# State products of a chunked scan, and the spread of 1 / rms, in float32r passes of heads and rests

## The chip, the cores and the metric

The kernel runs on one core of one Trainium2 chip. It is one program with one launch. The metric is the device time of that core in microseconds; the median of three runs before the change is 1921.77 us. A core has TensorE (PE in the profile, with PEld for its weight loads), VectorE (DVE), ScalarE (ACT), GpSimd (POOL), and SyncE (SP), which issues most DMAs. PE multiplies out of SBUF into PSUM banks of 512 fp32 columns on 128 partitions.

## The reference

One layer of a hybrid decoder, in fp32, on a prompt of 16 meta tokens and 1024 tokens and on eight samples of one token each:

```python
h = h + 0.5 * swiglu(rmsnorm(h, n1), w1g, w1u, w1d)
u = rmsnorm(h, nm) @ w_in
q, fz, iv, g, z, xbc, dt_raw = jnp.split(u, SPLITS, axis=-1)
...
o_hg, s_hg = run_segments(hgrn2_chunked, HG_CHUNK, segs, ...)
...
y, s_ssm = run_segments(partial(ssd_chunked, a_neg=a_neg), SSM_CHUNK, segs, ...)
...
h = h + jnp.concatenate([o_hg, yz], axis=-1) @ w_out
h = h + 0.5 * swiglu(rmsnorm(h, n2), w2g, w2u, w2d)
```

Two pieces of it matter here. The first is the norm ahead of the first FFN, `y = x * rsqrt(mean(x * x) + EPS) * w`, one factor 1 / rms per token. The second is the step of the Mamba-2 scan over chunks of 128 tokens:

```python
def step(h, inp):
    xc, dtc, bc, cc = inp
    cum = jnp.cumsum(dtc * a_g, axis=1)
    ...
    y = jnp.einsum('bgts,bgrts,bsgr,bsgrp->btgrp', cb, seg, dtc, xc)
    y = y + jnp.einsum('btgn,bgrpn,btgr->btgrp', cc, h, jnp.exp(cum))
    last = cum[:, -1]
    h = (h * jnp.exp(last)[..., None, None]
         + jnp.einsum('bsgn,bsgr,bsgrp->bgrpn', bc, dtc * jnp.exp(last[:, None] - cum), xc))
    return h, y
```

There are 8 heads of 64 columns in 2 groups, and a state of 128. The sum with `bc` in the last line is the state product.

## The kernel before

The 1048 tokens lie along the free axis, in four quarters of Q = 262 columns, and the features on partitions. The five stages follow each other on PE: first FFN, input projection with both scans laid into it, output projection, second FFN, final norm.

Nearly all products of the large weights are made by `mm3`: each operand is a float32r head (a rounded copy) and a float32r rest (operand minus head), and a product is three passes into the same PSUM bank, head by head, head by rest, rest by head (L169, L170, L171). Heads of weights are cast on ACT, rests are subtracted on DVE (`split`, L163 and L164; L497 and L501 in the FFNs). A smaller number of products is made in plain fp32, which the profile counts as two records each on PE. Among them are the spread of 1 / rms and everything in the Mamba-2 scan.

Buffers: slots "u" (30) and "s" (8, of 1056 columns) for large tiles, tiles "t" (9, of 524 columns, used as fp32), PSUM banks "mis" (4, in rotation through `psm`) and "acc" (4) for the large products.

**The norm in the first FFN.** Here the factor 1 / rms isn't applied to x ahead of the products; it is multiplied into their results. `Input.rms` computes it for each token with tokens on partitions: `st[:, 1]` holds ten columns, one for each tile of 128 tokens (the last has fewer; `tiles` lists start and count). What the FFN needs is a tile whose every partition holds the factors along the free axis, the spread. For this ACT scales the identity by each of the ten columns (L1425), which gives a diagonal of 1048 columns in a "u" slot, and `spread_r(q)` multiplies a matrix of ones with a quarter of it (L1430, one fp32 product of 262 columns for each q) and copies the bank to SBUF on ACT (L1431). The FFN's products are a numbered list of steps; `before(S, i, ...)` puts other work ahead of step i, and `spread_r(q)` stands ahead of step 28 + q. L704 and L705 later consume a spread quarter on DVE and ACT.

**The scan.** `ssm_scan` handles nine chunks c, eight of 128 tokens and one of 16. `front(c)` prepares, `back(c, hT)` consumes, and `fill(n)` issues n steps of the input projection, each three float32r passes of 344 to 350 columns, between them. After two fronts the loop is back(c), front(c + 2), fill(10). In `front`: a DMA brings the cumulated decays of eight heads, one row on all partitions, into a slot "s" (`mt`, L1612) and another brings `ec` (L1619); PE transposes x into bank px (L1622) and B into bank pb (L1630), and multiplies B by C into the other half of pb (L1632); DVE makes `xdt` (L1627), the masked product (L1633) and `xw` (L1641); ACT copies B transposed out of pb (`bt`, L1634) and turns `mt` into decays by eight Relus and an Exp (L1637, L1638); DVE multiplies these by the masked product (L1640, two instructions); ACT applies Exp to `ec` (L1643). In `back`: C by the state into bank pi (L1654), which DVE multiplies into `ec` (L1655); the y product from `xdt` and `mt` into bank py (L1659), added by DVE (L1662); the state product from `bt` and `xw` into bank ps, two fp32 products of 128 x 256 (L1665); the old state by its decay (L1670) and the sum (L1671) on DVE; the skip term (L1674). So a chunk takes five "mis" banks of four.

The order of PE's instructions in this part is the one written in the code. The order on the other engines is decided by a scheduler from the program's dependences.

Of the kernel before, what the change touches and what calls it, by code (L numbers as in the profile page):

```python
# [9 lines left out]
F32 = mybir.dt.float32  # L10
F32R = mybir.dt.float32r
U8 = mybir.dt.uint8
AF = mybir.ActivationFunctionType
# [4 lines left out]
P = 128  # L18
# [6 lines left out]
T = TP + NS  # L25
# [3 lines left out]
Q = T // 4  # L29
# [38 lines left out]
class Core:  # L68
# [45 lines left out]

    def t(self, w=CW):
        t = self.tmp.tile([P, 2 * Q], F32, tag="t", name=self.uid("t"), bufs=9)
        return t[:, :w]

    def raw(self, w=512):
# [175 lines left out]
class Spread:  # L295
# [14 lines left out]
    def lanes(self, n, cs):  # L310

        return self.tile().rearrange("p (c n t) -> p n c t", c=2, n=2)[:, n, cs]
# [896 lines left out]
def constants(K, a):  # L1209
    nc = K.nc  # L1210
    cst = K.const
    K.ident = cst.tile([P, P], F32, name="ident")
    make_identity(nc, K.ident)
    K.ones = {}
    for n in (1, D):
        K.ones[n] = cst.tile([P, P], F32, name=f"ones{n}")
        nc.vector.memset(K.ones[n], 1.0 / n)
    K.eps = cst.tile([P, 1], F32, name="eps")
    nc.vector.memset(K.eps, EPS)
    K.lna = cst.tile([P, 1], F32, name="lna")  # L1220
    nc.vector.memset(K.lna, -math.log(2.0) / 3.0)
# [85 lines left out]
class Input:  # L1307
# [111 lines left out]
    def rms(self):  # L1419

        K = self.K
        token_rstd(K, *(self.st[:, j] for j in range(3)))
        self.diag = K.slot("u", T)
        for i, (t0, n) in enumerate(self.tiles):
            K.nc.scalar.activation(self.diag[:, t0 : t0 + n], K.ident[:, :n], AF.Identity, scale=self.st[:, 1, i : i + 1])  # L1425

    def spread_r(self, q):
        K = self.K
        ps = K.psm()[:, :Q]
        K.nc.tensor.matmul(ps, K.ones[1], self.diag[:, q * Q : q * Q + Q], start=True, stop=True)  # L1430
        K.nc.scalar.copy(self.spread.quarter(q), ps)  # L1431


def token_rstd(K, v, r, q):

    token_sqrt(K, v, r)
    token_newton(K, v, r, q)
# [162 lines left out]
def ssm_scan(K, a, o, fill):  # L1600
    nc = K.nc
# [3 lines left out]
    state = {}  # L1605

    def front(c):

        t0, n = CT[c]
        r8 = slice(8 * c, 8 * c + 8)  # L1610
        mt = K.slot("s", w=1024).rearrange("p (h t) -> p h t", h=8)
        nc.sync.dma_start(mt[:, :, :n], K.cumd[r8, :n].partition_broadcast(P))  # L1612
        tk = K.pack()
        ec, bt, cbm = tk.tile([P, 4, P]), tk.tile([P, 256]), tk.tile([P, 2, P])
        cs = slice(t0, t0 + n)
        if c > 0:

            for f in range(2):
                nc.sync.dma_start(ec[64 * f : 64 * f + 64, :, :n], K.cumd[8 * c + f : 8 * c + 8 : 2, :n].partition_broadcast(64))  # L1619
        px = K.psm()  # L1620
        for j in range(4):
            nc.tensor.transpose(px[:n, j * P : (j + 1) * P], xs[j][:, cs], K.ident)  # L1622
        xx = K.slot("s", w=1024)
        xdt = xx[:, 0:512]
        xw = xx[:, 512:1024]
        pxv = px[:n].rearrange("p (h d) -> p h d", h=8)
        nc.vector.tensor_mul(xdt[:n].rearrange("p (h d) -> p h d", h=8), pxv, K.dt[:n, r8][:, :, None].broadcast_to([n, 8, 64]))  # L1627
        pb = K.psm()
        for g in range(2):
            nc.tensor.transpose(pb[:n, g * P : (g + 1) * P], B[g][:, cs], K.ident)  # L1630
        for g in range(2):
            nc.tensor.matmul(pb[:n, 256 + g * P : 256 + g * P + n], B[g][:, cs], C[g][:, cs], start=True, stop=True)  # L1632
        nc.vector.tensor_mul(cbm[:n, :, :n], pb[:n, 256:512].rearrange("p (g t) -> p g t", g=2)[:, :, :n], K.tri[:n, None, :n].broadcast_to([n, 2, n]))  # L1633
        nc.scalar.copy(bt[:n], pb[:n, 0:256])  # L1634

        for hh in range(8):
            nc.scalar.activation(mt[:n, hh, :n], mt[:n, hh, :n], AF.Relu, scale=-1.0, bias=K.cum[:n, 8 * c + hh : 8 * c + hh + 1])  # L1637
        nc.scalar.activation(mt[:n, :, :n], mt[:n, :, :n], AF.Exp, scale=-1.0)  # L1638
        for g in range(2):
            nc.vector.tensor_mul(mt[:n, 4 * g : 4 * g + 4, :n], mt[:n, 4 * g : 4 * g + 4, :n], cbm[:n, g, None, :n].broadcast_to([n, 4, n]))  # L1640
        nc.vector.tensor_mul(xw[:n].rearrange("p (h d) -> p h d", h=8), pxv, K.wdec[:n, r8][:, :, None].broadcast_to([n, 8, 64]))  # L1641
        if c > 0:
            nc.scalar.activation(ec[:, :, :n], ec[:, :, :n], AF.Exp)  # L1643
        state[c] = mt, ec, bt, xdt, xw

    def back(c, hT):
        t0, n = CT[c]
        r8 = slice(8 * c, 8 * c + 8)
        cs = slice(t0, t0 + n)
        mt, ec, bt, xdt, xw = state.pop(c)  # L1650
        if c > 0:
            pi = K.psm()
            for j in range(4):
                nc.tensor.matmul(pi[:, j * P : j * P + n], hT[:, j * P : (j + 1) * P], C[j // 2][:, cs], start=True, stop=True)  # L1654
            nc.vector.tensor_mul(ec[:, :, :n], pi.rearrange("p (j t) -> p j t", j=4)[:, :, :n], ec[:, :, :n])  # L1655
        py = K.psm()
        for hh in range(8):
            j, f = divmod(hh, 2)
            nc.tensor.matmul(py[64 * f : 64 * f + 64, j * P : j * P + n], xdt[:n, 64 * hh : 64 * hh + 64], mt[:n, hh, :n], start=True, stop=True)  # L1659
        pyv = py.rearrange("p (j t) -> p j t", j=4)  # L1660
        if c > 0:
            nc.vector.tensor_add(ec[:, :, :n], pyv[:, :, :n], ec[:, :, :n])  # L1662
        ps = K.psm()
        for g in range(2):
            nc.tensor.matmul(ps[:, 256 * g : 256 * g + 256], bt[:n, g * P : (g + 1) * P], xw[:n, 256 * g : 256 * g + 256], start=True, stop=True)  # L1665
        hn = hbuf[c % 2]
        if c == 0:
            nc.scalar.copy(hn, ps)
        else:
            nc.vector.tensor_mul(hn.rearrange("p (h d) -> p h d", h=8), hT.rearrange("p (h d) -> p h d", h=8), K.ecl[:, r8][:, :, None].broadcast_to([P, 8, 64]))  # L1670
            nc.vector.tensor_add(hn, hn, ps)  # L1671
        for j in range(4):
            yj = ec[:, j, :n] if c > 0 else pyv[:, j, :n]
            nc.vector.scalar_tensor_tensor(xs[j][:, cs], xs[j][:, cs], K.dcol[:, j : j + 1], yj, ALU.mult, ALU.add)  # L1674
        return hn

    fill(14)
    front(0)
    fill(6)
    front(1)  # L1680
# [544 lines left out]
def body(ctx, tc, a, o):  # L2225
    nc = tc.nc
    K = Core(ctx, tc)
# [6 lines left out]
    x = Input(K, a, wn1, ops, spread)  # L2234

    def before(S, i, *fns):
        for fn in fns:
            S.before(i, (lambda fn=fn: fn[0](*fn[1:])))

    def first1(S, w, w2):  # L2240
# [73 lines left out]
        before(S, 27, (e.low, 5), (e.cast, 7))  # L2314
        before(S, 28, (e.low, 7))
        for q in range(4):
            before(S, 28 + q, (x.spread_r, q))
        before(S, 33, (e.cast, 4))
        before(S, 34, (e.low, 4))

# [59 lines left out]
    with K.tc.manual_schedule(engines={mybir.EngineType.PE}):  # L2380
# [9 lines left out]
        for hd in range(NH):  # L2390
# [4 lines left out]
            g = us[hd]["g"] if hd < 3 else None  # L2395
# [29 lines left out]
    for k in range(KT):  # L2425
        t = K.slot("s", TO)
# [141 lines left out]
```

## Time and profile before

| | before |
|---|---|
| three runs, us | 1921.77, 1921.94, 1921.77 |
| profiled execution, us | 1922.67 |
| its span, us | 1920.9 |
| mean granted PE clock | 0.998 |
| PE idle while the scan runs (814 to 886 us), by the windows | 0.04 us |
| the four spread products, from the last pass ahead of them to the first one behind, us | 59.77 to 68.92 |

The span is the time from the first to the last instruction on the core; the time of a run has a little more around it. A row of a timeline is start, duration, engine, line, operation, output and inputs by the program's names, shapes and count; in brackets stands the idle time of the engine ahead of it and what ended it. PE's instructions are pipelined, so their durations overlap, and the time that one occupies PE is read from the distance between starts. Rows of PEld are the weight loads that run ahead of the matmuls. A row of the groups by line ends with the busy time, the mean duration in ns, and the idle time ahead of it.

### The profile page before, as it was taken

How to read it: one execution, taken by the hardware profiler on the slowest of the kernel's cores; microseconds unless marked ns; L12 is line 12 of the kernel's file. 1: busy time of each engine (PE TensorE's matmuls, PEld its weight loads, DVE VectorE, ACT ScalarE, POOL GpSimd, SP SyncE). 2: the span in 40 equal slices, each digit the busy share in tenths (PEclk: the TensorE clock that was granted, in tenths of full speed). 3: DMA queues.
4: the chain of work that ended last, by engine and by line, in shares of the span. 5: the costliest groups of instructions: out<-in, count | busy, mean ns of one | idle time of the engine just before them, and what ended most of it. 6: DMA issues, size and time to landing. Idle time of an engine off the chain costs nothing.

```text
span 1920.9 us, 41195 instructions
## 1 busy us (share of the span) xinstructions
PE 1905.5 (99%) x16692; PEld 1875.2 (98%) x16692; DVE 1526.5 (79%) x2866; ACT 858.0 (45%) x1635; POOL 30.1 (2%) x88
## 2 busy tenths in 40 slices
PE   9999999999999999999999999999999999999998
PEld 9999999999999999999999999999999999999998
DVE  7888888889788877566585557999888888978974
ACT  6533333334534644466564545743333332453353
POOL 3000000000000000000000000000000000000000
PEclk9999999999999999999999999999999999999999
DMA  7143333335967541221463254133333333596852
GB/s 249 50 128 95 95 107 112 92 98 175 305 215 243 165 152 52 66 89 38 116 186 85 83 173 144 58 114 107 99 93 101 101 112 93 173 269 210 281 175 84
DMA packets 324209, 258.46 MB, mean 135 GB/s; under 512 B 18923, under 2 KB 298731, under 8 KB 324011
## 3 DMA queue, kind: packets, MB, share of 16 engines
q1 hardware_dynamic: 323779, 255.79, 43.1%
q8 instruction: 131, 2.15, 0.5%
q14 instruction: 59, 0.48, 0.1%
q0 software_dynamic: 224, 0.04, 0.0%
q10 hardware_dynamic: 16, 0.00, 0.0%
HBM read 190.79 MB, written 65.05 MB: 133 GB/s over the span
## 4 chain that ended last, share of the span: by engine, by line
PE 94%; DVE 3%; ACT 1%; issue 1%; DMA 0%; SPq 0%; DVEq 0%; ACTq 0%
PE acc L169 24%; PE acc L171 23%; PE acc L170 23%; PE mis L169 5%; PE mis L170 5%; PE mis L171 5%; PE mis L1963 1%; DVE u L382 1%; DVE u L367 1%; PE mis L1665 0%; PE mis L2030 0%; PE mis L1659 0%; DMA s<-in_x_prompt_dram 0%; PE mis L2055 0%; PE mis L1654 0%
## 5 line engine op out<-in xcount | busy, mean ns | idle before, releaser
L169 PE MATMUL acc<-u,ws 128*128 128x258 f32 (+4 forms) x3634 | 1064.0, 293 | 1.1 <-DVE u L1279 0.8
L171 PE MATMUL acc<-u,ws 128*128 128x258 f32 (+4 forms) x3634 | 1055.3, 290 | 0.7 <-DVE ws L501 0.7
L170 PE MATMUL acc<-u,ws 128*128 128x258 f32 (+4 forms) x3634 | 1054.8, 290 | 0.0
L169 PEld LDWEIGHTS acc<-u,ws 128*128 128x128 f32 x3634 | 686.5, 189 | 8.7 <-issue 6.2
L170 PEld LDWEIGHTS acc<-u,ws 128*128 128x128 f32 x3634 | 688.3, 189 | 0.8 <-DVE u L330 0.2
L171 PEld LDWEIGHTS acc<-u,ws 128*128 128x128 f32 x3634 | 686.1, 189 | 1.6 <-DVE ws L501 1.1
L169 PE MATMUL mis<-u,ws 128*128 128x262 f32 (+1 forms) x810 | 230.2, 284 | 0.0
L171 PE MATMUL mis<-u,ws 128*128 128x262 f32 (+1 forms) x810 | 228.7, 282 | 0.0
L170 PE MATMUL mis<-u,ws 128*128 128x262 f32 (+1 forms) x738 | 208.6, 283 | 0.0
L501 DVE TENSOR_TENSOR ws<-r,ws 128x512 fp32r<-128x512 f32 x266 | 181.6, 684 | 4.1 <-ACT ws L497 3.9
L901 ACT ACTIVATE t<-t 128x524 f32<-128x524 f32 (+1 forms) x72 | 46.1, 640 | 300.1 <-DVE t L898 300.1
L497 ACT CAST ws<-r 128x512 fp32r<-128x512 f32 x266 | 156.8, 615 | 42.2 <-PE mis L171 18.1
L169 PEld LDWEIGHTS mis<-u,ws 128*128 128x128 f32 x810 | 152.9, 189 | 0.1
L171 PEld LDWEIGHTS mis<-u,ws 128*128 128x128 f32 x810 | 152.7, 189 | 0.0
L170 PEld LDWEIGHTS mis<-u,ws 128*128 128x128 f32 x738 | 139.9, 190 | 0.1
L493 DVE TENSOR_TENSOR r<-r,r 128x512 f32<-128x512 f32 x150 | 100.8, 684 | 0.3
L1031 DVE TENSOR_TENSOR u<-u,u 128x1048 fp32r<-128x1048 f32 (+3 forms) x84 | 96.1, 1146 | 4.8 <-ACT u L1027 4.3
L1089 ACT CAST ws<-u 128x512 fp32r<-128x512 f32 (+1 forms) x72 | 42.1, 585 | 109.9 <-DVE u L1084 105.2
L164 DVE TENSOR_TENSOR ws<-r,ws 128x512 fp32r<-128x512 f32 x88 | 59.5, 685 | 38.3 <-ACT ws L163 38.0
L1027 ACT CAST u<-u 128x1048 fp32r<-128x1048 f32 (+3 forms) x84 | 82.8, 988 | 1.3 <-DMA u<-hd 1.3
L1118 DVE SCALAR_TENSOR_TENSOR s<-acc,s 128x524 f32<-128x524 f32 (+3 forms) x86 | 53.9, 651 | 35.3 <-PE acc L171 35.0
L898 DVE TENSOR_TENSOR t<-t,u 128x524 f32<-128x524 f32 (+1 forms) x108 | 73.2, 692 | 0.1
(465 smaller groups left out, 2329.1 us busy)
## 6 DMA issues: line engine op xcount, KB each, us to landing
r<-in_w_ffn_down_dram SPq DMA_DIRECT2D x128, 256.0 KB
hd<-s SPq DMA_DIRECT2D x93, 258.0 KB
r<-in_w_ffn_gate_dram SPq DMA_DIRECT2D x88, 256.0 KB
r<-in_w_ffn_up_dram SPq DMA_DIRECT2D x88, 256.0 KB
hd<-s SPq DMA_DIRECT2D x77, 262.0 KB
u<-hd SPq DMA_DIRECT2D x36, 516.0 KB
u<-hd SPq DMA_DIRECT2D x28, 524.0 KB
r<-in_w_in_dram SPq DMA_DIRECT2D x56, 256.0 KB
```

Source lines behind the costliest of these rows:

```text
L164: self.nc.vector.tensor_sub(lo, src, hi.bitcast(F32))
L169: mm(ps, whi, xhi, start=first, stop=False, skip_group_check=more)
L170: mm(ps, whi, xlo, start=False, stop=False, skip_group_check=more)
L171: mm(ps, wlo, xhi, start=False, stop=last, skip_group_check=more)
L493: self.K.nc.vector.tensor_tensor(self.raw[p], self.raw[x], self.raw[y], op)
L497: self.K.nc.scalar.copy(self.w[p][:, : self.n * P], self.raw[p])
L501: self.K.nc.vector.tensor_sub(t[:, 512 : 512 + w], self.raw[p], t[:, :w].bitcast(F32))
L898: nc.vector.tensor_mul(t, t if src is None else src, spread.lanes(n, slice(0, 2)))
L901: nc.scalar.activation(t, t, AF.Silu)
L1027: K.nc.scalar.copy(hi, lo.bitcast(F32))
L1031: K.nc.vector.tensor_sub(lo, lo.bitcast(F32), hi.bitcast(F32))
L1118: nc.vector.scalar_tensor_tensor(t, b, 0.5, t, ALU.mult, ALU.add)
```

## The change

It edits two places. In the scan, `bt`'s head and rest lie side by side in one "t" tile declared float32r (`tr`), the rest by a new DVE subtraction out of pb; `xw` is split into `xh` (ACT) and `xl` (DVE), each in a "t" tile; and the state product is `mm3` for each of the two groups, six float32r passes of 256 columns. In the first FFN, the ten scaled identities go. The ten columns of 1 / rms are split into heads and rests in one small tile (`parts`, two DVE operations), and a spread quarter is made of passes with a column of `parts`, repeated over 128 columns, as weights, and of columns of a float32r identity (`identr`, cast once on DVE at the start) as the moving side: for each piece of a token tile in the quarter one pass for the head and one for the rest, 24 in all. They stand ahead of step 29 + q.

```diff
+    def tr(self, w=512):
+        t = self.tmp.tile([P, 2 * Q], F32R, tag="t", name=self.uid("t"), bufs=9)
+        return t[:, :w]
...
+    K.identr = cst.tile([P, P], F32R, name="identr")
+    nc.vector.tensor_copy(K.identr, K.ident)
...
-        self.diag = K.slot("u", T)
-        for i, (t0, n) in enumerate(self.tiles):
-            K.nc.scalar.activation(self.diag[:, t0 : t0 + n], K.ident[:, :n], AF.Identity, scale=self.st[:, 1, i : i + 1])
+        self.parts = K.sml.tile([P, 2, 10], F32R, tag="rp", name="rp", bufs=1)
+        K.nc.vector.tensor_copy(self.parts[:, 0], self.st[:, 1])
+        K.nc.vector.tensor_sub(self.parts[:, 1], self.st[:, 1], self.parts[:, 0].bitcast(F32))
 
     def spread_r(self, q):
         K = self.K
         ps = K.psm()[:, :Q]
-        K.nc.tensor.matmul(ps, K.ones[1], self.diag[:, q * Q : q * Q + Q], start=True, stop=True)
+        for i, (t0, n) in enumerate(self.tiles):
+            c0, c1 = max(t0, q * Q), min(t0 + n, q * Q + Q)
+            for j in range(2):
+                if c0 < c1:
+                    K.nc.tensor.matmul(ps[:, c0 - q * Q : c1 - q * Q], self.parts[:, j, i : i + 1].broadcast_to([P, P]), K.identr[:, c0 - t0 : c1 - t0], start=j == 0, stop=j == 1)
         K.nc.scalar.copy(self.spread.quarter(q), ps)
...
-        ec, bt, cbm = tk.tile([P, 4, P]), tk.tile([P, 256]), tk.tile([P, 2, P])
+        ec, cbm = tk.tile([P, 4, P]), tk.tile([P, 2, P])
+        bt, xh, xl = K.tr(), K.tr(), K.tr()
...
-        nc.scalar.copy(bt[:n], pb[:n, 0:256])
+        nc.scalar.copy(bt[:n, 0:256], pb[:n, 0:256])
+        nc.vector.tensor_sub(bt[:n, 256:512], pb[:n, 0:256], bt[:n, 0:256].bitcast(F32))
...
+        K.split(xw[:n], xh[:n], xl[:n])
...
         for g in range(2):
-            nc.tensor.matmul(ps[:, 256 * g : 256 * g + 256], bt[:n, g * P : (g + 1) * P], xw[:n, 256 * g : 256 * g + 256], start=True, stop=True)
+            gs, xs_ = slice(g * P, g * P + P), slice(256 * g, 256 * g + 256)
+            K.mm3(ps[:, xs_], bt[:n, gs], bt[:n, 256 + g * P : 256 + g * P + P], xh[:n, xs_], xl[:n, xs_], True, True)
...
-            before(S, 28 + q, (x.spread_r, q))
+            before(S, 29 + q, (x.spread_r, q))
```

The line numbers grow by the change: L1622 becomes L1633, L1630 L1641, L1640 L1652, L1641 L1653, L1655 L1668, L1659 L1672, L1430 L1440, and the passes of `mm3` become L173 to L175.

PE at the first spread quarter; `mis_886` and `mis_893` are its bank, the other rows are the FFN's passes. Before:

```order
L169 MATMUL mis_871<-u_438,ws_609 128x262
L170 MATMUL mis_871<-u_491,ws_609 128x262
L171 MATMUL mis_871<-u_438,ws_609 128x262
L1430 MATMUL mis_886<-u_814,ones_83 128x262
L169 MATMUL acc_825<-u_526,ws_628 128x262
```

With the change:

```order
L173 MATMUL acc_819<-u_528,ws_630 128x262
L174 MATMUL acc_819<-u_546,ws_630 128x262
L175 MATMUL acc_819<-u_528,ws_630 128x262
L1440 MATMUL mis_893<-identr,rp 128x128 x4
L1440 MATMUL mis_893<-identr,rp 128x6 x2
L173 MATMUL acc_833<-u_528,ws_647 128x262
```

One product is six passes, and it stands behind all twelve passes of the next step.

PE in a middle chunk of the scan, from the last pass of a fill over C by the state (`u`, `s`) and the y product to the state product. Before:

```order
L171 MATMUL acc_10355<-u_8548,ws_10069 128x350
L1654 MATMUL mis_10368<-u_9776,s_9903 128x128 x2
L1654 MATMUL mis_10368<-u_9877,s_9903 128x128 x2
L1659 MATMUL mis_10374<-s_10203,s_10213 64x128 x8
L1665 MATMUL mis_10384<-s_10213,s_10205 128x256 x2
```

With the change:

```order
L175 MATMUL acc_10411<-u_8562,ws_10095 128x350
L1667 MATMUL mis_10424<-u_9790,s_9917 128x128 x2
L1667 MATMUL mis_10424<-u_9891,s_9917 128x128 x2
L1672 MATMUL mis_10430<-s_10243,s_10256 64x128 x8
L173 MATMUL mis_10440<-t_10247,t_10246 128x256
L174 MATMUL mis_10440<-t_10248,t_10246 128x256
L175 MATMUL mis_10440<-t_10247,t_10246 128x256
```

The last three come once more, for the second group. Nothing else moves here: six passes that read "t" tiles stand where the two fp32 products stood.

DVE in the same part, from the two multiplications of a front (xdt and xw, out of px) to the two additions of the back behind it. Before:

```order
L1627 TENSOR_TENSOR s_10314<-mis_10309,s_8936 128x512
L1641 TENSOR_TENSOR s_10314<-mis_10309,s_8936 128x512
L1670 TENSOR_TENSOR s_9903<-s_9903,s_8936 128x512
L164 TENSOR_TENSOR ws_10529<-r_10527,ws_10529 128x512
L1640 TENSOR_TENSOR s_10304<-s_10304,s_10306 128x512 x2
L1655 TENSOR_TENSOR s_10205<-mis_10368,s_10205 128x512
L1662 TENSOR_TENSOR s_10205<-mis_10374,s_10205 128x512
L1671 TENSOR_TENSOR s_9903<-s_9903,mis_10384 128x512
```

With the change:

```order
L1646 TENSOR_TENSOR t_10357<-mis_10369,t_10357 128x256
L1638 TENSOR_TENSOR s_10367<-mis_10362,s_8950 128x512
L1653 TENSOR_TENSOR s_10367<-mis_10362,s_8950 128x512
L1684 TENSOR_TENSOR s_9917<-s_9917,s_8950 128x512
L168 TENSOR_TENSOR ws_10600<-r_10598,ws_10600 128x512
L168 TENSOR_TENSOR ws_10605<-r_10603,ws_10605 128x512
L1652 TENSOR_TENSOR s_10354<-s_10354,s_10356 128x512 x2
L168 TENSOR_TENSOR t_10359<-s_10367,t_10358 128x512
L1668 TENSOR_TENSOR s_10245<-mis_10424,s_10245 128x512
L1685 TENSOR_TENSOR s_9917<-s_9917,mis_10440 128x512
L1675 TENSOR_TENSOR s_10245<-mis_10430,s_10245 128x512
```

New are the rest of bt (L1646) and the rest of xw (L168 into a "t" tile). The latter stands between L1652, which was L1640, and L1668, which was L1655; it does so in this chunk, the one ahead and the one behind, and in no other chunk do these three follow each other so. The sum into the state (L1685) and the addition of y (L1675) have changed places.

More of the change, by code (lines that the diff above doesn't have):

```diff
@@ L1641, in front @@
         nc.vector.tensor_mul(xw[:n].rearrange("p (h d) -> p h d", h=8), pxv, K.wdec[:n, r8][:, :, None].broadcast_to([n, 8, 64]))
+        K.split(xw[:n], xh[:n], xl[:n])
         if c > 0:
             nc.scalar.activation(ec[:, :, :n], ec[:, :, :n], AF.Exp)
-        state[c] = mt, ec, bt, xdt, xw
+        state[c] = mt, ec, bt, xdt, xh, xl
     def back(c, hT):
@@ L1649, in back @@
         cs = slice(t0, t0 + n)
-        mt, ec, bt, xdt, xw = state.pop(c)
+        mt, ec, bt, xdt, xh, xl = state.pop(c)
         if c > 0:
```

## The prediction

> **What bounds the kernel now.** I read the page first: shares of busy time, then the chain that ended last.
>
> ```profile
> span 1920.9 us, 41195 instructions
> PE 1905.5 (99%) x16692; PEld 1875.2 (98%) x16692; DVE 1526.5 (79%) x2866; ACT 858.0 (45%) x1635; POOL 30.1 (2%) x88
> PE 94%; DVE 3%; ACT 1%; issue 1%; DMA 0%; SPq 0%; DVEq 0%; ACTq 0%
> ```
>
> TensorE (PE) is busy for 99% of the span, and the chain runs through it for 94%. So an edit pays by the PE time that it takes out, and costs by the PE idle time that it makes. The list of what PE waited for tells how little idle time there is to win.
>
> ```profile
> PE mis L1343 <- DMA s<-in_x_prompt_dram: 2.1, 2, 1.9
> PE acc L105 <- DVE ws L101: 1.5, 1, 1.5
> ```
>
> These lead that list and lie in the load at the start, which the change leaves alone. Of the rest only this group, from the groups by line and shape, belongs to what it edits: 0.9 us of waiting, last column.
>
> ```profile
> L1430 PE MATMUL mis<-u,ones 128*128 128x262 f32 x8 | 2.6, 410 | 0.9 <-ACT u L1431 0.5 <-ACT u L1425 0.4
> ```
>
> The other place that it edits, the scan, was read from the table of nine-us windows and then from the timeline. Its fullest window:
>
> ```profile
> 868.00:877.00 9.00, 9.00 (x73) 8.55 (x74) 8.39 (x17) 8.22 (x15) 0.00 (x0) 1.00 0.27 89
> ```
>
> The columns behind the width are PE, weight loads, DVE, ACT, POOL. PE is full there, but DVE and ACT come within 0.6 and 0.8 us of it. Here work added on DVE and ACT can turn into a PE wait.
>
> **The state products.** One chunk on PE, in the timeline:
>
> ```profile
> 842.15 1.13 PE L1665 MATMUL mis<-s,s 128*128 128x256 f32 x4
> 843.12 0.60 PE L1622 MATMUL mis<-ident,u 128*128 128x128 f32 x4
> 843.56 0.41 PE L1630 MATMUL mis<-ident,u 128*128 128x128 f32 x2
> ```
>
> Records overlap, so I price by distance from start to start. Two fp32 products take 843.12 - 842.15 = 0.97 us. Six float32r passes of 256 columns replace them. The nearest row is the same kind of pass at 262 columns, in the first FFN:
>
> ```profile
> 59.77 0.28 PE L171 MATMUL mis<-u,ws 128*128 128x262 f32 x1
> 60.45 0.71 PE L1430 MATMUL mis<-u,ones 128*128 128x262 f32 x2 [0.40 <-ACT u L1425]
> 60.81 0.48 PE L169 MATMUL acc<-u,ws 128*128 128x262 f32 x1
> 61.12 0.29 PE L170 MATMUL acc<-u,ws 128*128 128x262 f32 x1
> ...
> 62.34 0.28 PE L171 MATMUL acc<-u,ws 128*128 128x262 f32 x1
> 62.46 0.60 PE L1430 MATMUL mis<-u,ones 128*128 128x262 f32 x2
> 62.71 0.48 PE L169 MATMUL acc<-u,ws 128*128 128x262 f32 x1
> 63.02 0.29 PE L170 MATMUL acc<-u,ws 128*128 128x262 f32 x1
> ...
> 68.92 0.28 PE L169 MATMUL acc<-u,ws 128*128 128x262 f32 x1
> ```
>
> From 61.12 to 62.34 lie ten passes, 0.122 us each. Six times that by 256/262 is 0.72, plus up to 0.1 for the turn from fp32 to float32r: a gain of 0.15 to 0.25 per chunk. I take 0.2, and for nine chunks (the last is as dear, its moving side being 256 wide too) **1.8 us** of PE.
>
> The new work lies on ACT and DVE. The rows nearest in shape:
>
> ```profile
> 859.77 0.63 ACT L163 CAST ws<-r 128x512 fp32r<-128x512 f32 x1
> 861.39 0.68 DVE L164 TENSOR_TENSOR ws<-r,ws 128x512 fp32r<-128x512 f32 x1
> 864.23 0.42 DVE L1633 TENSOR_TENSOR s<-mis,tri 128x256 f32<-128x256 f32 x1
> ```
>
> So a chunk adds 0.63 on ACT (xh) and 0.68 + 0.42 on DVE (xl, the rest of bt). bt's head was a copy before as well. None of the three is wanted soon: the state product that reads them comes a chunk later. By throughput there is room except in the window shown. What matters is who queues behind xl.
>
> That is L1655. It reads pi, and pi's PSUM bank (four in rotation, five taken per chunk) is the next one that pb's transposes (L1630) need. On DVE, L1655 stands behind L1640, which stands behind the Relu and Exp of a matrix that a DMA brings into the slot freed by the y product one chunk back. The loop, in rows:
>
> ```profile
> 850.03 1.09 PE L1659 MATMUL mis<-s,s 128*64 128x128 f32 x16
> 851.06 1.13 PE L1665 MATMUL mis<-s,s 128*128 128x256 f32 x4
> 851.22 0.33 SPq L1612 DMA_DIRECT2D s<-cumd  x1
> 855.36 0.40 ACT L1637 ACTIVATE s<-s,s 128x128 f32<-128x128 f32 x1 [4.87 <-DMA s<-cumd]
> 855.66 0.35 ACT L1634 COPY s<-mis 128x256 f32<-128x256 f32 x1
> 858.50 1.05 ACT L1638 ACTIVATE s<-s 128x1024 f32<-128x1024 f32 x1
> 859.58 1.29 DVE L1640 TENSOR_TENSOR s<-s,s 128x512 f32<-128x512 f32 x2 [2.93 <-ACT s L1638]
> 860.79 0.68 DVE L1655 TENSOR_TENSOR s<-mis,s 128x512 f32<-128x512 f32 x1
> 860.89 0.60 PE L1622 MATMUL mis<-ident,u 128*128 128x128 f32 x4
> 861.53 0.44 PE L1630 MATMUL mis<-ident,u 128*128 128x128 f32 x2
> PEld mis L1630 <- DVE s L1655: 0.3, 1, 0.3
> ```
>
> The y product ends at 851.06 and the loop lets L1630 go at 861.53: 10.47 us. By PE alone L1630 would come at 860.89 + 0.44 = 861.33 (four transposes took 843.12 to 843.56): 10.27. So the cover is already gone in this chunk, where L1630 waits 0.2 us; the last row, from the weight loads' waits, names the same wait and releaser.
>
> After the change PE's side of that race holds two state products, each 0.2 shorter: 10.27 - 0.4 = 9.87. The loop's side gains xl, 0.6 at DVE's distance (860.79 to 861.39 for an operation of 0.68), and loses some 0.2, since bt's copy (855.66) stands ahead of the Relus, in ACT's wait for the DMA: about 10.85. The order puts xl between L1640 and L1655 (there L1652 and L1668) in three consecutive chunks and in none of the others whose race is this close. A wait of 0.7 to 1.0 gives PE's side of the following chunk that much more, so every second one pays: two waits, 1.6 together. The 0.2 of before is taken off: **1.4 us** comes back. Bounds: none, if the DMA lands earlier or the scheduler's slack holds; three full waits, 3.0, if no chunk is relieved by the one ahead. Net of the scan: -1.8 + 1.4 = **-0.4**, between -2.3 (0.25 each, no wait) and +1.65 (0.15 each, three waits).
>
> The fills are queued behind a waiting L1630 on PE, and ACT and DVE get their drains later; nobody else waits. The tiles for bt, xh and xl come from a ring of nine that holds three chunks, and a chunk's are read at most two chunks after they are taken, so I cost the ring at nothing.
>
> **The spread.** From the last pass before it (59.77) to L169 at 68.92 are 9.15 us. That holds 49 distances of float32r passes, 49 x 0.122 = 5.98, so the four products with their waits cost 3.17. Where L1430 didn't wait it took 63.02 - 62.46 - 0.122 = 0.44; 4 x 0.44 = 1.76, and the rest, 1.4, is waiting for the diagonal (0.4) and for the copy L1431 (0.5, both in the group's row), with the restart behind each. Why both came late:
>
> ```profile
> 59.15 0.17 DVE L1451 TENSOR_TENSOR st<-st 128x10 f32<-128x10 f32 x1
> 59.41 2.84 ACT L1425 ACTIVATE u<-ident,st 128x128 f32<-128x128 f32 x10 [1.16 <-DVE st L1451]
> 64.58 0.38 ACT L1431 COPY u<-mis 128x262 f32<-128x262 f32 x1 [0.41 <-PE acc L171]
> 70.67 0.70 DVE L704 TENSOR_TENSOR t<-t,u 128x524 f32<-128x524 f32 x1
> ```
>
> Ten activations held ACT for 2.84 us. The change replaces them by two DVE operations of some 0.17 each (the L1451 row), ready by 59.8, and the first product moves one step, twelve passes or 1.5 us, later. Both waits go. What replaces the fp32 products is 24 small passes, 16.4 units of 128 columns if the narrow ones are added up. Their price has no row. Low end: streaming alone, 0.06 for 128 columns, 16.4 x 0.06 = 1.0. High end: fp32's price, 0.97 / 4 = 0.24 per 128 columns, 3.9. Each pass brings its own 128 columns of weights, as the transposes do, which have 128 columns too and run at 0.44 / 4 = 0.11; C·h, 16 columns wide in the last chunk, has a group of its own:
>
> ```profile
> L1654 PE MATMUL mis<-u,s 128*128 128x16 f32 x8 | 1.0, 252 | 0.0
> ```
>
> 8 records in 1.0 us, 0.125 each, however narrow. I take the transposes' 0.11: 24 x 0.11 = 2.64, a gain of 3.17 - 2.64 = **0.5 us**; by the ends +2.2 and -0.7. The last copy, to end near 69.5, is wanted by L704 at 70.67: the step's delay costs nothing, and a copy later than that would push the DVE chain behind it. The float32r identity is one more cast on DVE in the load at the start, where the first products wait for DMA; at nothing, and 0.2 us if that cover is gone.
>
> The Trainium skill bears on the price of these passes: "TensorE: Matmul & The Clock Gate", section "LDWEIGHTS (loading the stationary operand)", gives a load as its columns / 1.2 ns, whatever the rows. An estimate by it is 107 ns for 128 columns, 2.6 us for 24 loads. It speaks against splitting four products into 24, and the 0.11 of the transposes agrees with it.
>
> **Sum.** -0.4 - 0.5 = -0.9: span 1920.0. The runs' median 1921.77 stands 0.87 above the span of the profiled execution (1920.9), and I keep that distance: **1920.9 us**.
>
> **Rivals.** *All of PE's gain stays.* The loop doesn't get longer where it counts, since L1655 is released earlier by a Relu chain without bt's copy: -1.8 - 0.5, less the 0.2 wait that exists: 1919.3, and with every cheap end (0.25 per chunk, 2.2) 1917.1. For it: the wait stands once in the scan today. Against: the order has xl ahead of L1655 in the chunk behind that very one.
>
> *The small passes stream.* The loads hide fully and a 128-column pass costs 0.06: the spread gains 2.2 instead of 0.5, 1919.2. For it: 48 passes around it hide theirs under 262 columns. Against: 128-column transposes don't. The Trainium skill, same page, section "Weight-path perf modes — Fast Weight Load (FWL) and DoubleRow", has fast loads on for 128 weights of a type that isn't FP32; whether float32r counts no run here shows.
>
> *Slower: L1630's bank.* xl ahead of L1655 delays every chunk's transposes instead of every second of three. Seven boundaries at 0.6 are 4.2; -1.8 - 0.5 + 4.2 = +1.9: 1923.7. It decides from waits of 2.3 us in all, the two gains together. For it: DVE's 8.39 of 9 us in the window above, with 1.1 us per chunk to come. Against: in the other boundaries the order has L1655 first or PE's slack is larger.
>
> *Not what it says.* Passes from the new tiles run at fp32's price, 0.24 per 128 columns: six of them 2.9 instead of 0.97, nine chunks +17, 1938. The operand type is the one of the 262-column rows, so hardly.
>
> **How the numbers follow.** My forecast 0.58, all gain 0.17, streaming 0.09, slower 0.14, not what it says 0.02. A run of this kernel can tell about 0.2% from no change, 3.84 us: below 1917.9 or above 1925.6. Faster by that needs nearly every cheap end of two rivals at once: 0.07. Slower needs the bank wait at twice its price, or the last rival: 0.08. Same: 0.85. The range takes in streaming with most of the gain kept below, and the bank rival above: 1917.9 to 1924.0.
>
> **What would show it.** The six passes of a chunk at 0.12 from start to start, next transposes 0.7 to 0.8 after the first. At L1641 (L1630 before) waits on DVE L1668, two of 0.7 to 1.0 us and none elsewhere in the scan: right; none at all: the first rival; seven: the third. At L1440 no wait on ACT, 24 passes at 0.11: right; at 0.06 the second rival. PE idle outside of these two places, or another time for the other 1800 us, would show that I missed an effect.

## The result, and the profile after

| | before | after |
|---|---|---|
| median of 8 runs, us | 1921.77 (1920.91 to 1922.69) | 1928.02 (1925.08 to 1929.66) |
| ratio after / before, 95% interval | | 1.0031 [1.0020, 1.0042] |
| profiled execution and its span, us | 1922.67, 1920.9 | 1926.92, 1925.1 |

The change made the kernel 6.25 us slower, 0.3%. The forecast was 1920.9 us, and the range, 1917.9 to 1924.0, does not hold the result.

The page after, its first lines:

```profile
span 1925.1 us, 41283 instructions
PE 1906.6 (99%) x16726; PEld 1878.2 (98%) x16726; DVE 1535.1 (80%) x2887; ACT 860.6 (45%) x1634; POOL 32.6 (2%) x88
```

PE is busy for 1906.6 us instead of 1905.5, and the span is 4.2 longer, so most of the loss is PE standing still. The list of PE's waits says where (total, times, longest):

```profile
PE mis L1641 <- DVE s L1668: 4.1, 2, 2.5
PE mis L1349 <- DMA s<-in_x_prompt_dram: 2.1, 2, 1.8
PE acc L105 <- DVE ws L101: 1.5, 1, 1.5
```

The first row is new and is the wait that the prediction named: the transposes of pb, waiting for the bank that the product with the state holds, twice. The two behind it were there before, and the waits at the spread are gone from the list. The two edited places in PE's timeline; first the spread, its first and last product:

```profile
59.54 0.28 PE L175 MATMUL mis<-u,ws 128*128 128x262 f32 x1
...
61.00 0.28 PE L175 MATMUL acc<-u,ws 128*128 128x262 f32 x1
61.12 0.73 PE L1440 MATMUL mis<-identr,rp 128*128 128x128 f32 x6
61.71 0.37 PE L173 MATMUL acc<-u,ws 128*128 128x262 f32 x1
61.91 0.29 PE L174 MATMUL acc<-u,ws 128*128 128x262 f32 x1
...
67.49 0.73 PE L1440 MATMUL mis<-identr,rp 128*128 128x122 f32 x6
68.07 0.37 PE L173 MATMUL acc<-u,ws 128*128 128x262 f32 x1
```

From the last pass ahead of that step to the first behind the spread are 68.07 - 59.54 = 8.53 us, over the same 49 distances that took 9.15 before: 0.62 us gained. Then one chunk of the scan:

```profile
840.91 0.39 PE L173 MATMUL mis<-t,t 128*128 128x256 f32 x1
841.14 0.28 PE L174 MATMUL mis<-t,t 128*128 128x256 f32 x1
...
841.73 0.60 PE L1633 MATMUL mis<-ident,u 128*128 128x128 f32 x4
844.78 0.44 PE L1641 MATMUL mis<-ident,u 128*128 128x128 f32 x2 [2.45 <-DVE s L1668]
...
846.18 0.50 PE L173 MATMUL acc<-u,ws 128*128 128x350 f32 x1
846.47 0.49 PE L174 MATMUL acc<-u,ws 128*128 128x350 f32 x1
...
849.29 0.32 PE L175 MATMUL acc<-u,ws 128*128 128x350 f32 x1
849.45 0.32 PE L173 MATMUL acc<-u,ws 128*128 128x350 f32 x1
```

The state product takes 841.73 - 840.91 = 0.82 us instead of 0.97. Then pb's transposes wait 2.45 us. Behind the wait passes start every 0.29 us, and from 849.29 on every 0.16 as before it. The table of windows shows why (PE busy, granted clock):

```profile
844.00:846.00 2.00, 1.22 (x9) 0.93 0.45 136
846.00:848.00 2.00, 2.00 (x9) 0.50 0.00 0
848.00:850.00 2.00, 2.00 (x11) 0.71 0.00 0
```

The granted clock was at half for some 3.4 us, which cost about 1.7 us (the missing clock times the width of the windows: 0.14 + 1.0 + 0.58). The loop behind that wait, from the engines' timelines:

```profile
832.34 0.33 SPq L1622 DMA_DIRECT2D s<-cumd  x1
838.01 1.28 ACT L1649 ACTIVATE s<-s,s 128x128 f32<-128x128 f32 x4 [3.75 <-DMA s<-cumd]
841.15 1.04 ACT L1650 ACTIVATE s<-s 128x1024 f32<-128x1024 f32 x1
842.23 1.29 DVE L1652 TENSOR_TENSOR s<-s,s 128x512 f32<-128x512 f32 x2 [1.03 <-ACT s L1650]
843.44 0.68 DVE L168 TENSOR_TENSOR t<-s,t 128x512 fp32r<-128x512 f32 x1
844.04 0.68 DVE L1668 TENSOR_TENSOR s<-mis,s 128x512 f32<-128x512 f32 x1
```

Every member is the one that was predicted, xl (L168) ahead of L1668 too. But Relu came 838.01 - 832.34 = 5.67 us behind mt's DMA; before, it was 855.36 - 851.22 = 4.14. So 1.5 us of the wait are not xl's: the transfer landed later. Why it did is the question of most experiments.

### The profile page after: what moved, and what is told of

It is laid out like the page before. It is cut to its first block, busy times and chain, and to the rows that moved or that the text cites. A ratio compares the mean times of both kernels' runs of the same rounds, so it can differ in the third digit from the quotient of the medians.

```text
span 1925.1 us, 41283 instructions
## 1 busy us (share of the span) xinstructions
PE 1906.6 (99%) x16726; PEld 1878.2 (98%) x16726; DVE 1535.1 (80%) x2887; ACT 860.6 (45%) x1634; POOL 32.6 (2%) x88
## 3 DMA queue, kind: packets, MB, share of 16 engines
q8 instruction: 132, 2.16, 0.5%
## 4 chain that ended last, share of the span: by engine, by line
PE 95%; DVE 2%; ACT 1%; DMA 1%; issue 0%; SPq 0%; DVEq 0%; ACTq 0%
PE acc L173 24%; PE acc L175 24%; PE acc L174 24%; PE mis L173 6%; PE mis L175 6%; PE mis L174 6%; PE mis L1977 1%; DMA s<-cumd 1%; PE mis L2044 0%; DMA s<-in_x_prompt_dram 0%; PE mis L2069 0%; PE mis L1966 0%; PE mis L1672 0%; PE mis L2071 0%; PE mis L233 0%
## 5 line engine op out<-in xcount | busy, mean ns | idle before, releaser
L173 PE MATMUL acc<-u,ws 128*128 128x258 f32 (+4 forms) x3634 | 1064.2, 293 | 1.1 <-DVE u L1285 0.8
L175 PE MATMUL acc<-u,ws 128*128 128x258 f32 (+4 forms) x3634 | 1056.3, 291 | 0.6 <-DVE ws L505 0.6
L173 PEld LDWEIGHTS acc<-u,ws 128*128 128x128 f32 x3634 | 686.4, 189 | 8.6 <-issue 6.1
L175 PEld LDWEIGHTS acc<-u,ws 128*128 128x128 f32 x3634 | 685.7, 189 | 2.1 <-DVE ws L505 1.1
L175 PE MATMUL mis<-u,ws 128*128 128x262 f32 (+1 forms) x810 | 229.8, 284 | 0.0
L173 PE MATMUL mis<-u,ws 128*128 128x262 f32 (+1 forms) x810 | 229.7, 284 | 0.0
L173 PEld LDWEIGHTS mis<-u,ws 128*128 128x128 f32 x810 | 153.3, 189 | 0.0
L175 PEld LDWEIGHTS mis<-u,ws 128*128 128x128 f32 x810 | 152.7, 188 | 0.0
L168 DVE TENSOR_TENSOR ws<-r,ws 128x512 fp32r<-128x512 f32 x88 | 59.5, 687 | 38.3 <-ACT ws L167 35.7
```

The lines of the kernel that those rows point to most:

```text
L168: self.nc.vector.tensor_sub(lo, src, hi.bitcast(F32))
L173: mm(ps, whi, xhi, start=first, stop=False, skip_group_check=more)
L175: mm(ps, wlo, xhi, start=False, stop=last, skip_group_check=more)
```

## The experiments

Each kernel ran beside the kernel before on the same chip. The experiments came in four groups, on three chips; each group has its own median of the kernel before, and differences are taken against that.

**Each part alone.** `spread_only` is the change without its edits in `ssm_scan`; `scan_only` is the kernel before with those edits (and `tr`).

> The spread's part of the change alone, the scan as before. Theory (the loss lies in the scan; the spread gained what the marks 59.77 to 68.92 show, 0.6 us): 1921.2 us, 0.6 under the kernel before, and no wait at L1440. Rival (the 24 small passes or the later step cost time further on): 1923 or more.

> The scan's part alone, the spread as before. Theory: the whole loss and 0.6 us more than the full change, about 1928.5 us, with two waits of 1.5 to 2.5 us at pb's transposes and, behind the longer one, some 4 us at a lower granted PE clock. Rival (spread): between 1920 and 1922.

Measured beside 1922.07: the spread alone 1924.38, ratio 1.0014 [1.0005, 1.0023]; the scan's part alone 1921.89, ratio 1.0001 [0.9992, 1.0009]. The theory fell in both. The part that gains 0.6 us in its own place loses 2.3, and the part with the two waits loses nothing (its waits came to 1.1 us instead of 4.1). Together they should then lose 2.1, and lose 6.25. So the spread's edit does something to the scan, and something elsewhere as well.

**Does ec's DMA delay mt?** In the profile after, ec's DMA is issued 0.38 us behind mt's, and before it was 1.0. `xw_moved` and `xh_in_slot` move tiles between the rings to change just that:

```diff
 # xw_moved, from the kernel before
-        xw = xx[:, 512:1024]
+        xw = K.t(512)
 # xh_in_slot, from the kernel after
-        bt, xh, xl = K.tr(), K.tr(), K.tr()
+        bt = K.tr()
...
-        xx = K.slot("s", w=1024)
-        xdt = xx[:, 0:512]
-        xw = xx[:, 512:1024]
+        xx = K.slot("s", w=1024, dt=F32R)
+        xh, xl = xx[:, 0:512], xx[:, 512:1024]
+        xdt, xw = K.t(512), K.t(512)
```

> The kernel before, with xw in a tile t instead of in xdt's slot s; nothing is split, no work added. Theory (the DMA of ec is issued when the slot of xdt and xw is free; once xw doesn't hold it, right behind the DMA of mt, so both share the engines and mt lands 1.0 to 1.5 us later): ec's DMA 0.4 us behind mt's instead of 1.0, Relu 5.0 to 5.7 us behind mt's DMA instead of 3.7 to 4.1, and two waits of 1.2 to 1.7 us at pb's transposes: about 1924.5 us. Rival (xl in DVE's queue alone makes the waits): 1921.8 us, no new wait.

> The full change, but xh and xl lie in the slot s and xdt and xw in tiles t, so that the state product holds that slot again. The work is the same. Theory: ec's DMA 1.0 us behind mt's again, mt lands after 3.7 to 4.1 us, what is left is xl ahead of the product with pi in two chunks, one or two waits of 0.9 us, no lower clock: 1920.3 to 1921.2 us. Rival (xl in DVE's queue alone): as the full change, about 1928 us, waits of 1.6 and 2.5 us.

Measured beside 1922.07: `xw_moved` 1921.61, 0.9996 [0.9987, 1.0005]. Its ec came 0.37 us behind mt (833.85 and 834.22), and Relu 3.95 us behind mt's DMA, with no wait in the scan. `xh_in_slot`: 1923.56, 1.0010 [1.0001, 1.0019]; ec came 0.86 behind, and Relu 5.35 behind all the same, with two waits of 1.9 us together. Both point against the sharing of ec's DMA; that theory was dropped.

**Addresses.** The spread's edit also moves every slot "u" and "s". In the compiled program the new tile of 80 bytes per partition takes 96 and the float32r identity 512, so the slots begin 608 bytes further on, at addresses that are 0 modulo 64 instead of 32, while the weight tiles, which lie ahead of the small tiles, move by 512 alone. Four kernels separate this:

```diff
 # shift_96, from the kernel before, in Input.rms
+        pad = K.sml.tile([P, 20], F32, tag="rp", name="rp", bufs=1)
+        K.nc.vector.memset(pad, 0.0)
 # shift_512, from the kernel before, among the constants
+    pad = cst.tile([P, P], F32, name="pad")
+    nc.vector.memset(pad, 0.0)
 # full_128 from the kernel after, spread_128 from spread_only
-        self.parts = K.sml.tile([P, 2, 10], F32R, tag="rp", name="rp", bufs=1)
+        self.parts = K.sml.tile([P, 2, 16], F32R, tag="rp", name="rp", bufs=1)[:, :, 0:10]
```

> The kernel before, with one more tile of 80 bytes per partition in the pool of small tiles (one memset on DVE, read by nothing): all slots u and s move by 96 bytes, from addresses that are 32 modulo 64 to 0 modulo 64; what lies ahead of them stays. Theory (the new tile of heads and rests moves the slots, and float32r passes that read them are 0.27 ns slower each, and mt sometimes lands in a slot s after 5 us and more instead of 4): about 1924.5 us, 2.5 over the kernel before, the passes between 80 and 620 us at 121.94 ns from start to start instead of 121.68. Rival (something in the spread's own work or its step): 1922, as before.

> The kernel before, with one more tile of 512 bytes per partition among the constants: everything behind moves by 512 bytes, as the float32r identity moves it, and the slots stay at 32 modulo 64. Theory (what counts is the slots' place modulo 64): 1922 us, as before, passes at 121.68 ns. Rival (any shift of the addresses): 1924.5 us.

> The full change, its tile of heads and rests made 128 bytes wide instead of 80, so that the slots are at 32 modulo 64 again (640 bytes on from before); every instruction is the same. Theory: the passes are back at 121.68 ns, mt lands after 3.6 to 4.2 us, waits at pb's transposes about 1 us in all, no lower clock behind them: about 1921.3 us, 0.8 under the kernel before. Rival (the work itself costs the time): as the full change, 1928 us.

> The spread's part alone, its tile of heads and rests 128 bytes wide. Theory: 1921.4 us, 0.6 under the kernel before, passes at 121.68 ns. Rival: as with the tile of 80 bytes, 2.3 over the kernel before.

Measured beside 1921.67: 96 bytes cost 2.2 us (1923.83, 1.0011 [1.0002, 1.0019]), 512 bytes nothing that shows (1922.18, 1.0001 [0.9992, 1.0010]). With the tile of 128 bytes the full change took 1926.01 (1.0021 [1.0012, 1.0030]) and the spread alone 1924.15 (1.0013 [1.0004, 1.0022]). The place of the loss shows in the number of passes that PE fits into the same 540 us of the first FFN; the window of the kernel before, and of the kernel after:

```profile
80.00:620.00 540.00, 539.41 (x4429) 1.00 0.48 149
```

```profile
80.00:620.00 540.00, 539.49 (x4420) 1.00 0.49 149
```

Nine passes of 0.122 us fewer, 1.1 us, at the same clock and with the same idle time. `shift_96` had 4426, `shift_512` 4429, `full_128` 4431. It is the same in all kernels here that have the spread's edit, whose instructions don't depend on the tile's width: the four with the tile of 80 bytes have 4419 or 4420, the five with the tile of 128 bytes 4431 or 4432. Over the whole span, the distances between neighbouring passes of the large products, each set against the same one in the kernel before (those under 0.2 us in both), add up to 2.0 us more in `shift_96`, 2.1 in the kernel after, nothing in `shift_512` and 0.2 in `full_128`. So the addresses do slow the passes, and the wider tile takes it back. Which property of them counts is open: in the first FFN `shift_96` lost a third of what the kernel after lost, though the slots of both are at 0 modulo 64. The medians resolve two microseconds poorly: `spread_128` stands 2.5 above its kernel before, and `spread_only`, with the slower passes, 2.3 above its own. The rest of the theory fell: mt landed on time in `shift_96` (Relu 3.79 behind) and late in `full_128` (4.99) and `spread_128` (5.42). Lateness went with the spread's edit and not with the addresses.

**Packets of instructions.** The spread's edit has 24 passes, a load and a matmul each, in place of four fp32 products of two loads and two matmuls each: 32 more PE instructions ahead of the scan. Instructions come into the core by DMA too, on queues of their own: the page after has one with 132 packets and 2.16 MB, 16 KB each. `phase_more` and `phase_less` are to change nothing but the number of PE instructions ahead of everything, by way of the matmuls on a constant that only keep PE busy while the first loads land:

```diff
 # phase_more, from the kernel before
-        for _ in range(n):
-            self.nc.tensor.matmul(ps, c[:, :P], c, start=True, stop=True)
+        for _ in range(n if n < 14 else 2 * n):
+            w = 256 if n < 14 else P
+            self.nc.tensor.matmul(ps[:, :w], c[:, :P], c[:, :w], start=True, stop=True)
 # phase_less, from full_128: c and ps are 512 wide, and
-        for _ in range(n):
+        for _ in range(n // 2):
```

> The kernel before, with the 14 idle-time matmuls at the very start (256 columns, which only keep the PE clock up) made 28 of 128 columns: 28 PE instructions more ahead of everything, as the spread of the change brings 32 more, and nothing else. Theory (PE's instructions are fetched from memory in packets of 16 KB; with more of them ahead, the packet that comes about every second chunk falls into the first 3 us of the transfer of mt instead of behind it, and mt lands 1 us later): Relu 4.8 to 5.7 us behind mt's DMA in two or three chunks, and one to three waits at pb's transposes, 1 to 2.7 us together: 1923 to 1924.5 us. Rival (mt is late for another reason that the spread brings): mt lands as before, 1922 us, but for up to 1 us at the start.

> The full change with the slots back at 32 modulo 64 (tile of 128 bytes), and the matmuls that only keep the clock up made half as many of 512 columns: 26 PE instructions fewer ahead of everything, which takes back most of the 32. Theory: the packets of instructions fall behind mt's transfer again, mt lands after 3.6 to 4.2 us, waits at pb's transposes 1.1 us in all as in the scan's part alone: 1921 to 1922 us. Rival: as with the tile of 128 bytes alone, 1926 us, waits of 1.6 to 1.8 us.

Measured beside 1921.75: `phase_less` 1921.17, 0.9997 [0.9988, 1.0006]. Against `full_128` that is 4.9 us less, with the work unchanged and 15 matmuls, 30 instructions, fewer (the expectation miscounts them as 26). The start of one transfer of mt in `full_128`, from the timeline, and the DMA queues in the 3.5 us behind its issue (packets, MB, share of 16 engines):

```profile
832.42 0.33 SPq L1622 DMA_DIRECT2D s<-cumd  x1
837.41 1.28 ACT L1649 ACTIVATE s<-s,s 128x128 f32<-128x128 f32 x4 [3.17 <-DMA s<-cumd]
```

```profile
q1 hardware_dynamic: 380, 0.64, 61.6%
q8 instruction: 1, 0.02, 1.7%
```

The same two views of `phase_less`:

```profile
831.09 0.33 SPq L1622 DMA_DIRECT2D s<-cumd  x1
835.02 1.28 ACT L1649 ACTIVATE s<-s,s 128x128 f32<-128x128 f32 x4 [2.11 <-DMA s<-cumd]
```

```profile
q1 hardware_dynamic: 428, 0.66, 59.8%
```

One packet of instructions among mt's, Relu after 4.99 us; none, 3.93. PE's waits in the scan, of `full_128` and of `phase_less`:

```profile
PE mis L1641 <- DVE s L1668: 3.4, 2, 1.8
```

```profile
PE mis L1641 <- DVE s L1668: 1.0, 2, 0.7
```

These waits differ by 2.4 us and the medians by 4.9, with an interval of some 2.4 either way; the price of the packet is known no better than that.

In all 17 kernels with a profile I took the same transfer (the one issued between 829 and 835 us) and the same 3.5 us. In seven the instruction queue has a packet there (after, `spread_only`, `xh_in_slot`, `full_128`, `spread_128`, `phase_more`, `fill_first`), and Relu came 4.99 to 5.67 us behind; in the other ten it has none, and Relu came 3.69 to 3.95 behind. The other transfers in these windows don't make the split: q1's share is 51.6 to 61.6% in the seven and 49.0 to 68.2% in the ten. In the later transfers of the same kernels it is less clean. The second wait of the kernel after stands behind the transfer issued at 854.01, and in the 3.5 us behind that issue there is no packet; one starts just ahead of it (the last row is the queue between 853.75 and 854.00):

```profile
854.01 0.33 SPq L1622 DMA_DIRECT2D s<-cumd  x1
859.11 2.45 ACT L1649 ACTIVATE s<-s,s 128x128 f32<-128x128 f32 x8 [2.21 <-DMA s<-cumd]
q8 instruction: 1, 0.02, 31.8%
```

Thirteen later transfers have a packet that starts between 0.2 us ahead of the issue and 0.5 behind it: six were late (Relu after 4.86 to 5.74 us), seven were not (3.74 to 4.34). Packets that came 2.5 us or more behind the issue did no harm. So every late transfer that Relu waited for has a packet close to its issue, but such a packet does not always make one late.

`phase_more`, the opposite test, took 1926.53, 1.0023 [1.0014, 1.0032]: the packet appeared in the kernel before, Relu came 5.46 behind, and PE waited 1.1 us. But only that one transfer was late, and the median lost 4.8 us. Most of it goes to the edit's own matmuls at the start, in the kernel before and in `phase_more`:

```profile
1.49 3.36 PE L105 MATMUL acc<-ws 128*128 128x256 f32 x14 [1.49 <-DVE ws L101]
1.49 6.24 PE L106 MATMUL acc<-ws 128*128 128x128 f32 x28 [1.49 <-DVE ws L101]
```

The first product of the spread comes at 63.27 us there instead of 60.45. These 2.8 us and the wait make 3.9 of the 4.0 us between the two spans, so this run supports the cause and says little of its price.

**A control, and whether the two causes add up.** `before_wide`, `full_wide` and `spread_wide` are the kernel before, the kernel after and `spread_128` with the 512-column matmuls of `phase_less`.

> The kernel before, with only the wide clock-keeping matmuls (half as many of 512 columns, 26 PE instructions fewer ahead of everything). Theory (they matter by the place of the packets of instructions alone): between 1920.5 and 1922.5 us, and a packet within the first 3 us of a transfer of mt goes with Relu 4.8 us or more behind the DMA, none with 3.5 to 4.3. Rival (they gain by themselves, at the start): 1919 or less.

> The full change with its tile of 80 bytes, and the wide clock-keeping matmuls. Theory (the two causes add up): the slots' addresses cost 2 us, the rest as with the tile of 128 bytes and the wide matmuls: 1923.0 to 1924.0 us, passes at 121.94 ns between 80 and 620 us, waits of 1 us in all at pb's transposes. Rival (the width of the matmuls doesn't matter, or the address does it all): 1926 or more, or 1921.5.

> The spread's part alone, tile of 128 bytes, wide clock-keeping matmuls. Theory: no wait at pb's transposes over 0.5 us, mt after 3.5 to 4.3 us: 1921.2 us, 0.5 under the kernel before. Rival: 1924 us as without them.

Measured beside 1921.60: `before_wide` 1922.82, 1.0009 [1.0000, 1.0018]; `full_wide` 1922.85, 1.0005 [0.9997, 1.0014]; `spread_wide` 1921.43, 1.0000 [0.9991, 1.0009]. In none of the three was a transfer of mt late, and the spread alone lost its loss. The wide matmuls gain nothing by themselves; `before_wide` was 0.3 above what was expected, 1.2 above the kernel before, and why is not known. The full change in its four forms, difference of the medians to the kernel before in us:

| | tile of 80 bytes | tile of 128 bytes |
|---|---|---|
| 30 matmuls of 256 columns at the start | +6.25 (the change) | +4.34 (`full_128`) |
| 15 of 512 columns | +1.25 (`full_wide`) | -0.58 (`phase_less`) |

The addresses cost 1.9 in the first line and 1.8 in the second, the packets 5.0 in the first column and 4.9 in the second. That is what two causes that add up would give. Each of these differences has an interval of some 2.5 us either way, so the medians alone show the packets' price and not the addresses', and that the pairs agree to 0.1 is partly luck. What is left of the change without either is -0.6, which is not told apart from nothing.

**The wait taken out of the way.** `fill_first` is `full_128` with four of a chunk's ten fill steps between `back` and `front`; `before_fill_first` is the kernel before with the same.

```diff
         if c + 2 < NC:
+            fill(4)
             front(c + 2)
...
-        fill(10 if c + 1 < NC else 6)
+        fill((6 if c + 2 < NC else 10) if c + 1 < NC else 6)
```

> The full change with the tile of 128 bytes, and four of the ten fill steps of a chunk put between back and front, so that pb's transposes come 1.9 us later in PE's order. Theory (all that is lost in the scan is lost at that one wait): waits of 0 to 0.5 us in all, whenever mt lands; the gain of 1.8 us in the state products and 0.6 us in the spread stays: 1919.5 to 1920.5 us. Rival (the chunk's loop is bound by DVE and ACT, and the wait moves to another instruction): 1924 us or more, waits at the y product or at the product with the state.

> The kernel before with the same four fill steps put between back and front. Theory: it loses its wait of 0.2 us and nothing else changes: 1921.5 us, within 0.5 of the kernel before. Rival (the place of the fills helps by itself): 1920.5 or less.

Measured beside 1921.75: `fill_first` 1921.38, 0.9998 [0.9990, 1.0007]; `before_fill_first` 1921.36, 0.9999 [0.9990, 1.0008]. In `fill_first` mt was still late (Relu 5.28 behind), and the wait is all but gone:

```profile
PE mis L1641 <- DVE s L1668: 0.2, 1, 0.2
```

4.7 us against `full_128` come from moving that one wait, with the packet still there. The waits became 3.2 us shorter, and the 4.7 has an interval of some 2.4 either way, so as far as the runs can tell the packet's price is paid at pb's bank. It did not reach the 1919.5 to 1920.5 us that were expected: no gain shows beside the scatter of the runs, and no version measured here beats the kernel before by more than its interval.

## Why the prediction was wrong

- *What bounds the kernel* held. PE's share stayed at 99%, and what was lost was PE's time.
- *The price of the state products* was too high a gain: 0.97 to 0.82, 0.15 per chunk, the low end, since the first float32r pass behind the fp32 ones takes 0.23 (840.91 to 841.14). At that price nine chunks gain 1.35 instead of 1.8.
- *The spread* was right. 0.62 measured, 0.5 forecast: no wait is left, and the passes take (8.53 - 49 x 0.122) / 24 = 0.106 us each on the mean, where 0.11 was taken. The rival in which they stream at 0.06 is out. By the rule of the Trainium skill, "TensorE: Matmul & The Clock Gate", section "LDWEIGHTS (loading the stationary operand)", columns / 1.2, a load of 128 columns is estimated at 107 ns. The 106 ns measured here agree with it.
- *The loop* was right in its members, its releaser (L1668), the order behind xl and the number of its waits, two. **The step that failed is the loop's length, "about 10.85".** It was made from the one loop of the trace of before with xl added, and took the 4.14 us from mt's DMA to Relu as fixed. They became 5.67 and 5.10 in the two loops that waited, and the waits 2.45 and 1.60 instead of 0.7 to 1.0. Without the 1.53 and 0.96 us by which the transfers were later, the waits would be 0.92 and 0.64, about the forecast. The runs showed the cause at work in the place of a packet of instructions, which the prediction did not look at: the spread's edit, 770 us ahead, lengthened PE's program by 32 instructions. The bound of three full waits, 3.0, was the mechanism's own size and left the transfer out.
- *The range* lacked a second thing: the step that costs the new tiles and the identity at nothing counted a cast and a ring, and not where the slots lie afterwards. That is 2.1 us by the passes of the profiled execution and 1.9 by the medians, and no wait shows it.
- *The rival on the other side*, L1630's bank in every boundary, was the right place by the wrong road: two boundaries and not seven, each dearer. It named 1923.7; 1928.0 was measured.
- *What would show it* was met in part: the two waits stand at L1641 alone, and there was "another time for the other 1800 us", as the sign of an effect missed.

The measured time is 7.1 us above the forecast. The waits are 2.5 of it (4.1 instead of 1.6), the addresses 1.9 and the state products 0.45. The remaining 2.2 are not shown: the half clock behind the longer wait cost 1.7 in the profiled execution, but the kernel before has such a stretch elsewhere, and the scatter of the medians is as large.

Left open: why a packet of instructions delays a transfer by more than its own share (its place in the same 16 engines is argued, not shown), and why it did so in some transfers and not in others; which property of the addresses slows the passes; and why `before_wide` lost 1.2 us that its profile does not show.

## What to carry to other kernels

A loop through a DMA that has no slack left is priced with the transfer's late landings and not with the one in the trace: here 1 us of lateness was paid in full, and moving four fill steps ahead of the waiting transposes took it away whatever was late. An edit has a length in instructions and a size in bytes besides its work; where a kernel is bound to 0.1%, a padded tile and an unchanged instruction count are the control that tells the work's effect from these two. Parts of a change that are measured alone need not add up, and when they do not, the question is what one does to the other's place in time.

## What was not expected of the hardware

- With one packet of instructions of 16 KB 0.9 to 1.9 us behind its issue, the transfer of 512 KB named above let its reader start after 4.99 to 5.67 us instead of 3.69 to 3.95 (7 and 10 kernels). With the packet nearer to the issue, six of thirteen transfers were late.
- Float32r passes in the first FFN fitted 4420 times or 4429 times into 540 us, by where the slots begin. Moved by 96 bytes alone, the slots gave 4426 there and 2.0 us more over the whole span; moved by 512, no difference.
- Apart from the last microseconds, nine of the 17 profiled executions had one stretch of half clock, about 3.4 us long, in one of four places: at the start, behind the tiny matmuls near 747 us, behind the scan near 896, or behind the wait of 2.45 us above (none behind a wait of 1.8 in `full_128`). In the profiled execution of the kernel before it is here:

```profile
746.00:748.00 2.00, 2.00 (x16) 0.85 1.02 289
748.00:750.00 2.00, 2.00 (x9) 0.50 0.36 90
750.00:752.00 2.00, 2.00 (x12) 0.79 0.85 242
```

  The missing clock is 0.30 + 1.0 + 0.42 = 1.7 us, and the kernel after does not have it there. Single executions therefore differ by such an amount in one place or another, and total times were compared by medians.
